# Moving the begin of 24 background weight-sum transfers out of the output projection

## The chip, the cores and the metric

The kernel runs on one core of a Trainium2 chip. The metric is the device time of one execution in microseconds. It is judged over several runs; one more execution was taken with the hardware profiler, and all rows below come from that one.

## The reference

One layer of a streaming encoder on x (1024 rows, 1024 columns, float32). Every product is done in float32 accuracy.

```python
h = rms_norm(x, ln1_g)
z = h @ w_in                         # columns for three mixers
y = concat(short_conv(...),          # gated 3-tap convolution, 256 columns
           diff_attention(...),      # 4 heads, block-causal, 512 columns
           gla(...))                 # gated linear attention, 4 heads, 256 columns
x = x + y @ w_out                    # output projection, 1024 x 1024
h2 = rms_norm(x, ln2_g)
x = x + square(relu(h2 @ w_mlp1)) @ w_mlp2    # 1024 -> 4096 -> 1024
```

## The kernel before

A float32 product is done as three fp32r products: `split` (L135) casts a tile to its high part on ScalarE (L136) and subtracts it from the original on VectorE for the low part (L137); `mm3` (L155) multiplies low by high, high by high, high by low. The two MLP products are done by a seven-product scheme on 2 x 2 blocks, in which the weight operand of a product is a block of w_mlp1 or w_mlp2 or a sum of such blocks. The sums don't depend on x. They are made by DMA alone, from DRAM to DRAM: one transfer copies 1 MB of a block, a later one adds 1 MB of another block onto it with `accum_op` (L116 and L119).

`BlockSums.steps()` (L111) is a generator over these transfers. For each of the two weights it gives 32 steps: 4 copies for sum 5, 4 copies for sum 2, 4 and 4 accumulations onto these, 4 copies and 4 accumulations for sum 4 (from sum 5), 4 copies and 4 accumulations for sum 1 (from sum 4). The copies for 5 and 2 read the weight, those for 4 and 1 read another sum. `sum_steps` (L125) chains the 32 of w_mlp1 and the 32 of w_mlp2, and the order is fixed. A step of w_mlp1 has rows of 8 KB, one of w_mlp2 rows of 2 KB.

`next_sum(when)` (L128) begins the next step: GpSimd copies one element of `when` into `paced`, which makes it wait until that element is written, and then issues the transfer from GpSimd's own queue (queue 0 in the profile). All other transfers are issued by SyncE, in order, on queue 1.

The stages, in order, and the steps that begin in each:

- The gate projection and the decay factors of the gated linear attention; the loop over 8 row tiles that makes `gv` (L354); its keys, states and queries. No steps.
- The gated linear loop, 16 iterations of `gla_scores` and `gla_out` (L497 to L501), with the projections of q, k and v for the first two attention heads interleaved (`steps01`). `gla_out` calls `next_sum` in each odd iteration: 8 steps.
- Four attention heads. Each calls `next_sum` after each of 8 query tiles (L609): 32 steps. Between the heads lie the projections that the next ones need.
- The convolution's projections, and the loads of y from DRAM (L671).
- The output projection (L724): four blocks of 256 columns of w_out, 8 row tiles each. A row tile is one `gemm_b` of 24 matmuls into a `ps_mm` bank (three of them), an addition to x1 on VectorE (L729) and a square with row sum on ScalarE (L730). In the first three blocks each row tile calls `next_sum` (L732): 24 steps. In the last block, each row tile is followed by `h2_tile` of that tile (norm, transposes, splits), and then come `h2_sums`.
- The first MLP product ("MLP 1", L831): 8 iterations of q, each with seven products of 24 matmuls each, their weight operands loaded by `w1_operand` (L757), two tiles of hidden units per iteration. No steps.
- The second MLP product (L928): seven terms in the order 5, 3, 7, 6, 4, 1, 2.

Weights are loaded by `load_w` (L139): two halves of 512 KB, each into a staging tile "st" (two of them, shared with `lp`, `g2` and the y loads), then split into tiles "hi" and "lo" (four each). `g2` (L698) is allocated in an "st" slot ahead of the output projection and read until the last `h2_tile`. A load waits for a free staging tile, a cast for a free hi tile. Tile's scheduler sets the order of each engine's instructions from a priority and its own model of times; dependencies become semaphore waits. `tc.issue_after` puts instructions of the same engine behind a given one.

Of the kernel before, what the change touches and what calls it, by code (L numbers as in the profile page):

```python
# [36 lines left out]
def hybrid_block(ctx, tc, x, ln1_g, w_in, conv_w, q_norm_g, k_norm_g, diff_lambda, diff_subln_g,  # L37
# [24 lines left out]
    def ps_tr():  # L62
        return psum.tile([P, 512], F32, name="ps_tr", tag="tr", bufs=2)
# [4 lines left out]
    def stage():  # L68
        return wpool.tile([P, 1024], F32, name="wst", tag="st", bufs=2)
# [58 lines left out]
    def next_sum(when):  # L128

        g = nc.gpsimd.tensor_copy(paced, when)  # L130
        with tc.issue_after(g.ins):
            next(sum_steps)


    def split(hi, lo, src):  # L135
        nc.scalar.copy(hi, src)  # L136
        return nc.vector.tensor_tensor(lo, src, hi.bitcast(F32), op=ALU.subtract)  # L137

    def load_w(w, c0, ncol):  # L139
        wb = []  # L140
        for kh in range(2):
            st = stage().rearrange("p (c n) -> p c n", c=4)
            wk = w[kh * 512:(kh + 1) * 512, :].rearrange("(c p) n -> p c n", p=P)
            nc.sync.dma_start(st, wk[:, :, c0:c0 + 256])
            hi = wpool.tile([P, 4, 272], F32R, name="whi", tag="hi", bufs=4)
            lo = wpool.tile([P, 4, 272], F32R, name="wlo", tag="lo", bufs=4)
            split(hi[:, :, 0:256], lo[:, :, 0:256], st)
            if ncol > 256:
                sx = c1.tile([P, 4, ncol - 256], F32, name="sx", tag="sx", bufs=2)
                nc.sync.dma_start(sx, wk[:, :, c0 + 256:c0 + ncol])  # L150
                split(hi[:, :, 256:ncol], lo[:, :, 256:ncol], sx)
            wb.append((hi, lo))
        return wb
# [19 lines left out]
    def gemm_b(wb, act, tt, ncol=256, ks=tuple(range(KC))):  # L173
        ps = ps_mm()
        th, o = tt // 4, (tt % 4) * P
        for kc in ks:
            hi, lo = wb[kc // 4]
            ah, al = act[th][kc // 4]
            mm3(ps[:, 0:ncol], ah[:, kc % 4, o:o + P], al[:, kc % 4, o:o + P],
                hi[:, kc % 4, 0:ncol], lo[:, kc % 4, 0:ncol], kc == ks[0], kc == ks[-1])  # L180
        return ps
# [29 lines left out]
    def g4(nm):  # L211
        return gp.tile([P, 1024], F32, name=nm, tag="g4", bufs=8)
# [110 lines left out]
    for j in range(4):  # L323
        ps = ps_s()
        for i in range(2):
            tt = 2 * j + i
# [13 lines left out]
    for pr in range(2):  # L340
        for th in range(2):
            ps = ps_s()
            for i in range(4):
                tt = th * 4 + i
# [8 lines left out]
    gv = r1.tile([P, NT, 256], F32, name="gv", tag="v")  # L353
    for tt in range(NT):  # L354
        ps = gemm_b(wb, hT, tt)
        nc.scalar.copy(gv[:, tt, :], ps[:, 0:256])
    wb = load_w(w_in, C_GK, 256)
    kE = [g4("kE") for _ in range(2)]
    for pr in range(2):
# [14 lines left out]
    for pr in range(2):  # L374
        nc.gpsimd.memset(S[pr][:, 0:64], 0.0)
        kv = [ps_s(), ps_s()]
        for c in range(15):
            tt, po = c // 2, (c % 2) * 64
# [82 lines left out]
    ssg = c1.tile([P, 32], F32, name="ssg")  # L461
# [12 lines left out]
    def gla_out(g):  # L474
        tt, hh = g // 2, g % 2
        po, att = hh * 64, attb[g % 4]
        ov = og[tt // 4][:, (tt % 4) * 256:(tt % 4) * 256 + 256].rearrange("p (r h e) -> p r h e", r=2, h=2)
        po_ = ps_tr()
        for pr in range(2):
            os_ = slice(pr * 64, (pr + 1) * 64)  # L480
            h0 = pr * P + hh * 64
            nc.tensor.matmul(po_[:, os_], att[:, pr, :], gv[:, tt, h0:h0 + 64], start=True, stop=False)
            for i in range(2):
                c = tt * 2 + i
                nc.tensor.matmul(po_[i * 64:(i + 1) * 64, os_],
                                 eb[pr][po:po + 64, c * 64:(c + 1) * 64],
                                 S[pr][po:po + 64, c * 64:(c + 1) * 64], start=False, stop=True)
        sq = gp.tile([P, P], F32, name="sqg", tag="sqg", bufs=2)
        nc.scalar.copy(ov[:, :, hh, :], po_[:, 0:P].rearrange("p (r e) -> p r e", r=2))
        nc.scalar.activation(sq, po_[:, 0:P], AF.Square)  # L490
        nc.vector.tensor_reduce(ssg[:, tt * 4:tt * 4 + 4].rearrange("p (r h) -> p r h", r=2)[:, :, hh],
                                sq.rearrange("p (r e) -> p r e", r=2), axis=AX.X, op=ALU.add)
        if g % 2 == 1:
            next_sum(ssg[0:1, tt * 4 + hh:tt * 4 + hh + 1])

    gla_scores(0)
    for g in range(2 * NT):  # L497
# [204 lines left out]
    ss2 = xp.tile([P, NT, 4], F32, name="ss2")  # L702

    def h2_tile(tt):
        r = norm_stats(ss2[:, tt, :], 4, xp)
        th, o = tt // 4, (tt % 4) * P
        osl = slice(o, o + P)
        for kh in range(2):
            ksl = slice(kh * 512, kh * 512 + 512)
            xn = xp.tile([P, 512], F32, name="xn", tag="xn", bufs=2)  # L710
            nc.vector.scalar_tensor_tensor(xn, x1[tt][:, ksl], r, g2[:, ksl], op0=ALU.mult, op1=ALU.mult)
            tp = ps_tr()
            for j in range(4):
                t_ = nc.tensor.transpose(tp[:, j * P:(j + 1) * P], xn[:, j * P:(j + 1) * P], ident)
            nc.scalar.copy(hb[th][kh][:, :, osl], tp.rearrange("p (c n) -> p c n", c=4))
        nc.sync.dma_start(x1d[tt], x1[tt])
        if th == 0:
            d6 = xp.tile([P, 4, P], F32, name="d6", tag="xn", bufs=2)
            nc.vector.tensor_tensor(d6, b11[:, :, osl], b21[:, :, osl], op=ALU.subtract)
            split(*[v[:, :, osl] for v in H[6]], d6)  # L720
            split(*[v[:, :, osl] for v in H[5]], b21[:, :, osl])
        return t_.ins

    for nb in range(4):  # L724
        wb = wo0 if nb == 0 else load_w(w_out, nb * 256, 256)
        for tt in range(NT):
            ps = gemm_b(wb, yT, tt, 256, (6, 7, 2, 3, 4, 5, 0, 1))
            xv = x1[tt][:, nb * 256:(nb + 1) * 256]
            nc.vector.tensor_tensor(xv, xv, ps[:, 0:256], op=ALU.add)  # L729
            nc.scalar.activation(ps[:, 0:256], xv, AF.Square, accum_out=ss2[:, tt, nb:nb + 1])  # L730
            if nb < 3:
                next_sum(ss2[0:1, tt, nb:nb + 1])  # L732
            if nb == 3 and tt < NT - 1:
                h2_tile(tt)

# [41 lines left out]
    def prods(q, i):  # L777
        w = w1_operand(q, i)
        return [prod(w, e, i, *BANKS[i]) for e in range(2)]
# [16 lines left out]
    def ftile(nm):  # L796
        return fp.tile([P, 512], F32, name=nm, tag=nm)
# [13 lines left out]
    def f_store(i, mp, r):  # L811
        nc.sync.dma_start(fdram[i][mp], r)
# [4 lines left out]
    def out65(mp, ps6, ps5):  # L817
        s6, s5, r5 = ftile("s6"), ftile("s5"), ftile("r5")
        nc.scalar.copy(s6, ps6)
        tadd(r5, ps5, s6)  # L820
        nc.scalar.copy(s5, ps5)
        relu2_v(r5)
        f_store(5, mp, r5)
        return s6, s5, r5
# [6 lines left out]
    for q in range(NQ):  # L831
        if q not in first:
            p6, p5 = prods(q, 6), prods(q, 5)
            first[q] = [out65(2 * q + e, p6[e], p5[e]) for e in range(2)]
        f = first.pop(q)
        p3 = prods(q, 3)
        s3s = []
        for e in range(2):
            s6, s5, r5 = f[e]
            s3 = ftile("s3")  # L840
            s3s.append(s3)
            nc.scalar.copy(s3, p3[e])
            tadd(s5, p3[e], s5, ALU.subtract)
        p7 = prods(q, 7)
        for e in range(2):
            s6, s5, r5 = f[e]
            tadd(s3s[e], p7[e], s3s[e])
            tadd(s6, s6, p7[e], ALU.subtract)
            relu2_s(s3s[e])
            f_store(3, 2 * q + e, s3s[e])  # L850
        p2 = prods(q, 2)
        for e in range(2):
            tadd(f[e][0], p2[e], f[e][0])
        p4 = prods(q, 4)
        for e in range(2):
            s6, s5, r5 = f[e]
            tadd(s6, p4[e], s6)
            tadd(s5, p4[e], s5)
            relu2_s(s6)
            f_store(7, 2 * q + e, s6)  # L860
        p1 = prods(q, 1)
        for e in range(2):
            s6, s5, r5 = f[e]
            s3, mp = s3s[e], 2 * q + e
            tadd(s5, p1[e], s5)
            relu2_v(s5)
            d6, d4, d2 = gtile(), gtile(), gtile()
            tadd(d6, s5, r5, ALU.subtract)
            f_store(6, mp, d6)
            tadd(s5, s5, s3, ALU.subtract)  # L870
            f_store(1, mp, s5)
            tadd(d4, r5, s5, ALU.subtract)
            f_store(4, mp, d4)
            tadd(d2, s6, d4, ALU.subtract)
            f_store(2, mp, d2)


    fp_cm.__exit__(None, None, None)
# [49 lines left out]
    for ip, (op, dests, done) in enumerate(plan):  # L928
        banks = [psum.tile([P, 512], F32, name="pso", tag=t, bufs=n) for t, n in sets[ip % 2]]
        for c in range(NC2):  # L930
            w, f = load2(op, c)
# [48 lines left out]
```

## Time and profile before

| | us |
|---|---|
| median of 3 runs | 1267.23 |
| lowest and highest of the runs | 1264.94, 1267.30 |
| the profiled execution, device time | 1265.83 |
| the profiled execution, span of its instructions | 1264.1 |

The span is what the rows below divide; all times of instructions count from its start. In a timeline row the first number is the start and the second the duration; in brackets stand the idle time of the engine before the instruction and what ended it. PE is TensorE's matmuls, PEld its weight loads, DVE VectorE, ACT ScalarE, POOL GpSimd, SP SyncE. A DMA issue takes part of a microsecond on the issuing engine; the transfer lands later.

### The profile page before, as it was taken

How to read it: one execution, taken by the hardware profiler on the slowest of the kernel's cores; microseconds unless marked ns; L12 is line 12 of the kernel's file. 1: busy time of each engine (PE TensorE's matmuls, PEld its weight loads, DVE VectorE, ACT ScalarE, POOL GpSimd, SP SyncE). 2: the span in 40 equal slices, each digit the busy share in tenths (PEclk: the TensorE clock that was granted, in tenths of full speed). 3: DMA queues.
4: the chain of work that ended last, by engine and by line, in shares of the span. 5: the costliest groups of instructions: out<-in, count | busy, mean ns of one | idle time of the engine just before them, and what ended most of it. 6: DMA issues, size and time to landing. Idle time of an engine off the chain costs nothing.

```text
span 1264.1 us, 17602 instructions
## 1 busy us (share of the span) xinstructions
PE 1197.6 (95%) x6803; PEld 1029.7 (81%) x6803; DVE 743.8 (59%) x1366; ACT 522.8 (41%) x1019; POOL 65.7 (5%) x147
## 2 busy tenths in 40 slices
PE   6999999999999999676689999999999999999998
PEld 6897899998988788576668888888888888888887
DVE  6616654568677873111597866776666555554553
ACT  6621233557566642111475343344433333333332
POOL 1000000020102112122000000000000000000000
PEclk8999999999999999778789999999999999999999
DMA  6211244197819778999734656565599995655000
GB/s 203 84 34 34 68 163 163 46 211 237 184 50 220 211 227 262 217 267 266 194 125 162 220 184 203 192 204 173 180 315 353 387 363 200 228 210 197 32 34 33
DMA packets 118961, 231.92 MB, mean 183 GB/s; under 512 B 7357, under 2 KB 53470, under 8 KB 115550
## 3 DMA queue, kind: packets, MB, share of 16 engines
q1 hardware_dynamic: 104286, 163.69, 38.1%
q0 software_dynamic: 14592, 67.11, 22.0%
q8 instruction: 53, 0.87, 0.3%
q14 instruction: 30, 0.25, 0.1%
HBM read 189.89 MB, written 108.00 MB: 236 GB/s over the span
## 4 chain that ended last, share of the span: by engine, by line
PE 78%; DMA 10%; DVE 6%; ACT 4%; issue 1%; SPq 1%; ACTq 0%; DVEq 0%
PE pso L158 8%; PE pso L156 8%; PE pso L157 8%; PE psp L156 8%; PE psp L157 8%; PE psp L158 8%; DMA wst<-in_w_out_dram 6%; PE ps_mm L156 6%; PE ps_mm L158 6%; PE ps_mm L157 6%; PE ps_av L605 3%; DMA wst<-in_w_mlp_dram 2%; PE ps_tr L597 1%; PE ps_s L575 1%; DMA wst<-ydram 1%; PE ps_s L576 1%
## 5 line engine op out<-in xcount | busy, mean ns | idle before, releaser
L157 PE MATMUL pso<-o2h 128*128 128x512 f32 x448 | 174.3, 389 | 0.0
L156 PE MATMUL pso<-o2l,o2h 128*128 128x512 f32 x448 | 174.3, 389 | 0.0
L158 PE MATMUL pso<-o2h,o2l 128*128 128x512 f32 x448 | 174.3, 389 | 0.0
L156 PE MATMUL ps_mm<-wlo,hTh 128*128 128x256 f32 (+1 forms) x512 | 147.8, 289 | 3.8 <-ACT hTh L201 3.8
L137 DVE TENSOR_TENSOR o2l<-f,o2h 128x1024 fp32r<-128x1024 f32 x56 | 68.6, 1225 | 139.4 <-ACT o2h L136 139.4
L157 PE MATMUL ps_mm<-whi,hTh 128*128 128x256 f32 (+1 forms) x512 | 147.1, 287 | 0.0
L158 PE MATMUL ps_mm<-whi,hTl 128*128 128x256 f32 (+1 forms) x512 | 146.2, 286 | 0.0
L136 ACT CAST o2h<-f 128x1024 fp32r<-128x1024 f32 x56 | 58.8, 1051 | 190.5 <-PE pso L157 186.6
L156 PE MATMUL ps_mm<-wlo,yTh 128*128 128x256 f32 x256 | 80.2, 313 | 32.5 <-ACT ps_mm L730 26.8
L137 DVE TENSOR_TENSOR wlo<-wst,whi 128x1024 fp32r<-128x1024 f32 x34 | 41.6, 1224 | 114.5 <-ACT whi L136 112.0
L136 ACT CAST w1h<-wst 128x1024 fp32r<-128x1024 f32 x56 | 58.9, 1053 | 106.8 <-PE psp L157 86.9
L156 PEld LDWEIGHTS ps_mm<-wlo,hTh 128*128 128x128 f32 x512 | 97.0, 190 | 7.0 <-ACT hTh L201 4.7
L157 PEld LDWEIGHTS pso<-o2h 128*128 128x128 f32 x448 | 84.1, 188 | 17.6
L158 PEld LDWEIGHTS pso<-o2h,o2l 128*128 128x128 f32 x448 | 84.1, 188 | 17.5
L156 PEld LDWEIGHTS pso<-o2l,o2h 128*128 128x128 f32 x448 | 84.1, 188 | 17.3
L158 PEld LDWEIGHTS ps_mm<-whi,hTl 128*128 128x128 f32 x512 | 97.4, 190 | 0.7 <-DVE hTl L202 0.2
L157 PEld LDWEIGHTS ps_mm<-whi,hTh 128*128 128x128 f32 x512 | 97.1, 190 | 0.9 <-issue 0.3
L815 DVE TENSOR_TENSOR s<-psp,s 128x512 f32<-128x512 f32 x96 | 64.7, 689 | 51.0 <-PE psp L158 46.0
L137 DVE TENSOR_TENSOR w1l<-wst,w1h 128x1024 fp32r<-128x1024 f32 x56 | 68.4, 1221 | 35.1 <-ACT w1h L136 35.1
L156 PEld LDWEIGHTS ps_mm<-wlo,yTh 128*128 128x128 f32 x256 | 55.5, 217 | 33.8 <-ACT ps_mm L730 27.9
L158 PE MATMUL ps_mm<-whi,yTl 128*128 128x256 f32 x256 | 78.3, 306 | 0.0
L157 PE MATMUL ps_mm<-whi,yTh 128*128 128x256 f32 x256 | 78.3, 306 | 0.0
(284 smaller groups left out, 2631.5 us busy)
## 6 DMA issues: line engine op xcount, KB each, us to landing
f<-fdram SPq DMA_DIRECT2D x28, 1024.0 KB
w1s<-in_w_mlp_dram POOLq DMA_DIRECT2D x24, 1024.0 KB, 9.8
w2s<-in_w_mlp_dram POOLq DMA_DIRECT2D x24, 1024.0 KB, 17.6
wst<-w1s SPq DMA_DIRECT2D x32, 512.0 KB
w<-w2s SPq DMA_DIRECT2D x16, 1024.0 KB
wst<-in_w_in_dram SPq DMA_DIRECT2D x26, 512.0 KB
wst<-in_w_mlp_dram SPq DMA_DIRECT2D x24, 512.0 KB
fdram<-s SPq DMA_DIRECT2D x48, 256.0 KB
```

The lines of the kernel that those rows point to most:

```text
L136: nc.scalar.copy(hi, src)
L137: return nc.vector.tensor_tensor(lo, src, hi.bitcast(F32), op=ALU.subtract)
L156: nc.tensor.matmul(ps, lh, rl, start=first, stop=False)
L157: nc.tensor.matmul(ps, lh, rh, start=False, stop=False)
L158: return nc.tensor.matmul(ps, ll, rh, start=False, stop=last)
L575: nc.tensor.matmul(ps[:, 0:w], qi, kll[c][:, j * 512:j * 512 + w], start=True, stop=False)
L576: nc.tensor.matmul(ps[:, 0:w], qi, khh[c][:, j * 512:j * 512 + w], start=False, stop=True)
L597: nc.tensor.transpose(tp[:, b * P:(b + 1) * P], pc[0][:, (b0 + b) * P:(b0 + b + 1) * P], ident)
L605: nc.tensor.matmul(av[:, 0:P], aT[:, b * P:(b + 1) * P], v[:, kb, hh * P:hh * P + P], start=(kb == 0), stop=(kb == i))
L815: nc.vector.tensor_tensor(dst, a_, b_, op=op)
```

## The change

The 24 calls of `next_sum` in the output projection are removed. 24 others are added: 8 in the loop that makes `gv`, one after each row tile's copy; 8 in the even iterations of the gated linear loop, which had them in the odd ones alone; and 8 in MLP 1, one at the end of each iteration of q. The element that paces a step of MLP 1 is one of r5 of the same iteration's first tile, which `out65` writes early in the iteration (for q of 0 and 1 ahead of the loop).

```diff
     for tt in range(NT):
         ps = gemm_b(wb, hT, tt)
         nc.scalar.copy(gv[:, tt, :], ps[:, 0:256])
+        next_sum(gv[0:1, tt, 0:1])
...
-        if g % 2 == 1:
-            next_sum(ssg[0:1, tt * 4 + hh:tt * 4 + hh + 1])
+        next_sum(ssg[0:1, tt * 4 + hh:tt * 4 + hh + 1])
...
             nc.scalar.activation(ps[:, 0:256], xv, AF.Square, accum_out=ss2[:, tt, nb:nb + 1])
-            if nb < 3:
-                next_sum(ss2[0:1, tt, nb:nb + 1])
             if nb == 3 and tt < NT - 1:
                 h2_tile(tt)
...
             tadd(d2, s6, d4, ALU.subtract)
             f_store(2, mp, d2)
+        next_sum(f[0][2][0:1, 0:1])
```

Since the order of the 64 steps is fixed, each stage gets other steps than before:

| stage | before | after |
|---|---|---|
| `gv` loop | none | 8 copies of w_mlp1 |
| gated linear loop | 8 copies of w_mlp1 | 8 accumulations, 4 copies from a sum, 4 accumulations of w_mlp1 |
| head 0 | 8 accumulations of w_mlp1 | 4 copies from a sum, 4 accumulations of w_mlp1 |
| head 1 | 4 copies from a sum, 4 accumulations of w_mlp1 | 8 copies of w_mlp2 |
| head 2 | 4 copies from a sum, 4 accumulations of w_mlp1 | 8 accumulations of w_mlp2 |
| head 3 | 8 copies of w_mlp2 | 4 copies from a sum, 4 accumulations of w_mlp2 |
| output projection | 16 accumulations, 8 copies from a sum of w_mlp2 | none |
| MLP 1 | none | 4 copies from a sum, 4 accumulations of w_mlp2 |

## Rows read from the trace of the kernel before

**Rows 1.** The page, its first line.

```profile
span 1264.1 us, 17602 instructions
```

**Rows 2.** The page, shares of the span in the chain that ended last.

```profile
PE 78%; DMA 10%; DVE 6%; ACT 4%; issue 1%; SPq 1%; ACTq 0%; DVEq 0%
```

**Rows 3.** That chain in order of time, 455 to 665 us: start, duration, what.

```profile
459.95 7.29 DMA wst<-ydram
...
481.68 3.75 DMA wst<-in_w_out_dram
...
487.85 18.66 DMA wst<-in_w_out_dram
...
508.91 11.98 DMA wst<-in_w_out_dram
...
611.86 1.05 ACT w1h L136
```

**Rows 4.** Waits, ScalarE 485 to 660, TensorE 485 to 615 us: total, times, longest.

```profile
ACT whi L136 <- DMA wst<-in_w_out_dram: 54.7, 6, 12.4
...
ACT w1h L136 <- DMA wst<-w1s: 9.9, 1, 9.9
...
PE ps_mm L156 <- ACT ps_mm L730: 26.8, 5, 7.0
```

**Rows 5.** Timelines of TensorE and ScalarE: projection's first matmul, 25th square.

```profile
480.21 0.27 PE L156 MATMUL ps_mm<-wlo,yTh 128*128 128x256 f32 x1
...
600.59 0.39 ACT L730 ACTIVATE ps_mm<-x 128x256 f32<-128x256 f32 x1 [1.27 <-DVE x L729]
```

**Rows 6.** Windows: length, PE, PEld, DVE, ACT, POOL busy (instructions), PEclk, DMA share, GB/s.

```profile
160.00:208.00 48.00, 48.00 (x407) 43.96 (x408) 24.25 (x62) 15.53 (x50) 4.48 (x11) 1.00 0.41 140
...
480.00:503.00 23.00, 23.00 (x194) 22.92 (x192) 6.43 (x12) 5.58 (x16) 6.95 (x12) 1.00 0.95 293
503.00:600.00 97.00, 64.47 (x438) 63.24 (x436) 13.78 (x24) 14.59 (x42) 17.15 (x35) 0.80 1.09 250
...
638.00:654.00 16.00, 10.47 (x54) 8.36 (x52) 16.00 (x38) 10.15 (x20) 0.00 (x0) 0.87 0.24 78
...
660.00:790.00 130.00, 130.00 (x569) 106.46 (x568) 93.73 (x126) 56.86 (x79) 0.00 (x0) 1.00 0.57 189
```

**Rows 7.** Timeline of GpSimd: first and last paced copy of eight, an accumulating step.

```profile
147.31 0.18 POOL L130 COPY paced<-ssg 1x1 f32<-1x1 f32 x1 [13.79 <-DVE ssg L491]
...
213.16 0.17 POOL L130 COPY paced<-ssg 1x1 f32<-1x1 f32 x1 [8.03 <-DVE ssg L491]
...
251.00 0.86 POOL L119 DMA_DIRECT2D w1s<-in_w_mlp_dram  x1 [0.27 <-issue]
```

**Rows 8.** DMA queues in 288:290, 292:294, 502:504 us: packets, MB, share of 16 engines.

```profile
q0 software_dynamic: 52, 0.39, 92.4%
q1 hardware_dynamic: 50, 0.10, 15.1%
...
q0 software_dynamic: 38, 0.20, 47.8%
...
q0 software_dynamic: 151, 0.30, 80.4%
q1 hardware_dynamic: 155, 0.16, 28.8%
```

**Rows 9.** Timeline of SyncE's queue: the issues of two v weights (two halves each).

```profile
169.99 3.19 SPq L144 DMA_DIRECT2D wst<-in_w_in_dram  x2
...
207.85 3.19 SPq L144 DMA_DIRECT2D wst<-in_w_in_dram  x2
```

**Rows 10.** Timeline of ScalarE: the first cast of each of these two weights.

```profile
205.52 1.05 ACT L136 CAST whi<-wst 128x1024 fp32r<-128x1024 f32 x1 [1.80 <-PE ps_mm L158]
...
233.07 1.05 ACT L136 CAST whi<-wst 128x1024 fp32r<-128x1024 f32 x1 [1.05 <-PE ps_mm L158]
```

**Rows 11.** Waits of ScalarE in MLP 1, 660 to 926 us.

```profile
ACT w1h L136 <- PE psp L157: 83.7, 47, 3.3
```

## The prediction

> **What bounds the kernel now.** I began with the page. The span is 1264.1 us [rows 1], and the chain that ended last is 78% TensorE and 10% DMA [rows 2]. A tenth of the span that waits for transfers in a kernel of matrix products is the thing to place, so I read the chain in order of time [rows 3]. Before 460 us it is TensorE, VectorE and ScalarE in turn. From 460 to 612 us it is almost nothing but loads: 7.29 us for a 512 KB piece of y, 3.75 us for the first w_out half that is loaded inside the stage, then 18.66, 11.98 and so on for halves of the same 512 KB. The reader is to see that one and the same kind of load takes 3.75 us once and 12 to 19 us afterwards.
>
> The waits say how this reaches TensorE [rows 4]. ScalarE stands before a cast of w_out for 54.7 us in six times, all on DMA, and 9.9 us once on an MLP operand. ScalarE works in order, so the squares of L730 stand behind such a cast; a square holds a PSUM bank of ps_mm, of which there are three; TensorE then waits for L730, 26.8 us in five times. The windows give the size [rows 6]: from 480 to 503 us TensorE is full (23.00 of 23 us, clock 1.00, 194 matmuls, so 0.1186 us each), from 503 to 600 us it has 64.47 of 97 us at a granted clock of 0.80. In that stretch DMA is at 1.09 and VectorE and ScalarE are below 15 us of 97. The projection is bound by its loads, and the loads by what shares the DMA engines: the 24 block sum steps that L732 issues.
>
> **What is removed.** The projection begins at 480.21 us [rows 5]. Were TensorE never short of weights, a row tile of one 256-column block is 24 matmuls of 0.1186 us, 2.85 us [rows 6]. ScalarE's cast at 611.86 us is the last that waits on a load [rows 3]; it is the second MLP operand's, and in ScalarE's order it stands behind the 25th square, which ran at 600.59 us [rows 5]. So I compare the time of that cast. Without competing transfers: 25 x 2.85 = 71.3 us brings the 25th tile to 551.5 us. The operand's own load can't begin earlier than the staging slot allows, and there is only one: g2 (L698) holds the other "st" slot through the whole stage. The first MLP operand is cast when the third block has freed its hi buffer, at 480.2 + 24 x 2.85 = 548.6 us; from there to the next issue it takes 2.4 us for cast and subtraction (the load issued at 487.85 us landed 18.66 us later, at 506.51, and the next was issued at 508.91 [rows 3]); then comes a load. For the load I take the 3.75 us of 481.68 us, which is the nearest uncrowded one of this very kind; the bound above is the 11.98 us of a crowded one. That gives 548.6 + 2.4 + 3.75 = 554.8 us, so 57.1 us are removed; 48.9 us with the bound above, and 60 us if the operand is there when the 25th tile is done.
>
> Do the other loads keep up, by the same price? A half costs 3.75 + 2.4 = 6.2 us, two halves 12.3 us, against 8 x 2.85 = 22.8 us of matmuls in a block. Yes, with 10 us over. The second half of block 1 is issued at 487.85 us behind eight x tiles, 4 MB on the same queue; it has until 503 us.
>
> From 612 us on the stage is the norm and the h2 sums. From 638 to 654 us VectorE is busy 16.00 of 16 us [rows 6], so this part doesn't shrink with faster loads. TensorE's clock there is 0.87, and full speed may give some 4 us in the 26 us ahead of it, an estimate from that clock; I take none.
>
> **What is added, stage by stage.** The order of the 64 steps is fixed, so 16 early begins shift everything behind them: the gv loop gets the 8 copies of w1's first two sums, the gated linear loop 8 accumulations, 4 copies and 4 accumulations of w1 where it had 8 copies, the attentions lighter and heavier mixes, MLP 1 the last 8 steps of w2.
>
> *Issue cost.* A step is a copy of one element and a DMA issue, under 1.4 us of GpSimd together, as the rows with POOL show [rows 7]. GpSimd has nothing else there that is waited for, so I put it at nothing; without that cover, 24 x 1.4 us = 34 us could be late, but only for other steps.
>
> *The gated linear loop.* In [rows 7] eight paced copies stand 9.4 us apart (147.31 to 213.16 us), so with twice as many a step will come every 4.7 us. An accumulation of w1 takes about 5.2 us of all DMA engines: the eight of head 0 were issued from 251.00 us and their queue runs empty in the window of 292 to 294 us [rows 7, 8]. The first eight therefore last from some 144 to 186 us; the next four from 199 to about 220 us. What suffers are the weight loads beside them. How much, a two-microsecond window shows: beside w1 accumulations queue 0 moved 52 packets and queue 1 moved 50, although those of queue 0 are 7.5 KB; beside w2 accumulations the counts are 151 and 155 [rows 8]. The two queues take turns by packet, whatever the size, so 1 KB packets of a load run at 25 per us beside w1 and 77 per us beside w2. The Trainium skill has this as a rule: in "DMA: Bandwidth & Descriptors", section "Queues, rings and completion order", each engine goes round its queue rows packet by packet. By that rule the trace agrees, and it speaks against this stage, since w1's packets are the largest that a load can meet.
>
> Worked out: the v load of pair 0 (two halves, 1024 packets) is issued from 169.99 us [rows 9]. Until 186 us it moves some 360 packets; the rest falls between copies and is through by about 190 us. Its cast comes at 205.52 us [rows 10]: 15 us to spare. The next pair's load, issued from 207.85 us [rows 9], moves 260 packets until 220 us and is through near 223 us; the cast is at 233.07 us [rows 10]: 10 us to spare. The four y stores of the loop queue behind it, and ScalarE may stand some 5 us before the third yt. Three ps_mm banks are 8.5 us of matmuls. So between nothing and 3 us; I take 1. TensorE is busy 48.00 of 48 us there now [rows 6], so any stall would be seen.
>
> *The attentions.* Head 0 and 1 get less accumulation than now. Head 3 now gets four accumulations as its last steps, where plain copies stood. They end later, and the y loads stand beside them: the 7.29 us load of 459.95 us [rows 3] already was beside copies. The last piece of y is needed almost when it arrives, so a delay goes to TensorE in full. Below: nothing, for the turns by packet cost 4 KB loads little. Above: two accumulations more to get past, 2 x 5.2 - 4 = 6 us. I take 1, nearer to nothing since the queues share.
>
> *MLP 1.* 569 matmuls in 130 us [rows 6] are 0.228 us each, so 5.5 us for an operand of 24. Eight steps are spread over some 270 us where DMA is at 0.57. The casts there wait for TensorE, not for loads: 83.7 us in 47 times [rows 11], so loads lie in their slots before a buffer is free, and four hi buffers are three operands, 16 us, ahead. A load beside a w2 accumulation takes 512/77 = 6.6 us plus its latency, about 8.7 us; that fits. Bounds 0 and 5 us; I take 0. The last sum is needed only by the sixth of the second product's seven terms.
>
> **Sum.** 57.1 - 1 - 1 = 55.1 us less. The profiled execution took 1265.83 us, so 1210.7; it lies between the lowest (1264.94) and the median (1267.23) of the runs. I say 1211 us.
>
> **Rivals.**
> *The receiving stages give back a part.* If accumulations ran without a gap, the two v loads would need 1024/25 = 41 us each: 3 us past the cast of the first pair and 16 us past the second's. With 6 us before the projection that is 25 us in place of the 2 I took, 1234 us. For it: the spare of 10 to 15 us rests on 5.2 us for an accumulation, against 4.7 us between steps. Against it: the loop's eight plus four accumulations end.
>
> *It doesn't do what it says.* One staging slot makes the loads a chain even alone. This decides once a half takes more than 22.8/2 - 2.4 = 9 us; at 11.98 us a block would take 28.8 us, and with halves as long as the 18.66 us behind x tiles 42.1 us. Three blocks of 42.1 us in place of 22.8 are 57.9 us, so the gain is gone and the time stays near 1266 us, within 0.2%; the x tiles and x1d stores would have to hold the loads there. Against it is the 3.75 us load. The Trainium skill's section "Issuing engines are not separate DMA queues" (same page) says that all such transfers share 16 engines, so the bytes are paid for somewhere; the windows show where there is room, 0.41 and 0.57 of DMA [rows 6].
>
> *Slower: MLP 1 stops on its casts.* There each operand's load is in ScalarE's order, as in the projection. If every one of the eight steps delayed one load from 3.75 to 11.98 us with no buffer between, 8 x 8.2 = 66 us would be lost, more than the 55 gained: 1277 us. It decides when the load's lateness exceeds the 16 us of operands ahead, or when ScalarE, held at a cast, keeps PSUM banks for over one product of 5.5 us. The 47 casts that wait for TensorE alone [rows 11] speak against it.
>
> **Chances.** The forecast 0.76, by itself 1204 to 1219 us; part given back 0.17; no gain 0.03; slower 0.04. A measurement of this kernel tells about 0.2% from no change: faster 0.93, same 0.03, slower 0.04. The ends: 60 us removed and nothing given back is 1206 us, 2 more from the clock 1204; 48.9 us removed and 9 given back (3 and 6; MLP 1 nothing) is 1226 us. I take 1204 to 1226 us, which leaves out the worse half of the second case and the last two.
>
> **What would show it.** Right: no wait of ScalarE on w_out over 4 us, squares 2.85 us apart through three blocks, granted clock near 1.00 from 480 to 550 us, second MLP operand cast near 555 us, MLP 1 steady some 55 us earlier. Gated linear loop: load casts still waiting for TensorE, with DMA near full to 186 us. Wrong: casts there or in MLP 1 that wait for DMA, TensorE idle before the projection, or loads of w_out still at 9 us or more.

## The result, and the profile after

The changed kernel takes 1223.72 us, the median of 4 runs (1220.67 to 1226.46), beside 1267.26 us for the kernel before beside it: a ratio of 0.966 with a 95% interval of 0.9634 to 0.9685. It is faster, by 43.5 us. The forecast was 1211 us with a range of 1204 to 1226 us, so the time lies inside the range and 12.7 us above the forecast. The profiled execution of the changed kernel took 1223.45 us.

The page of the kernel after, its first line and the shares of its chain, answers to [rows 1, 2]: transfers were 10% of the chain and are 3%.

```profile
span 1221.8 us, 17609 instructions
...
PE 85%; DVE 7%; ACT 3%; DMA 3%; issue 1%; SPq 1%; ACTq 0%
```

To see in which stage the time went I took landmarks that both kernels have. In the kernel after, these are the first and last starts of four groups of matmuls (duration minimum, median and maximum in ns; then first and last start in us):

```profile
L471 PE MATMUL ps_s<-eb,enb x64: 272/272/374, 141.8 to 206.9; 64*128 64x128 f32 x64
...
L575 PE MATMUL ps_s<-kll,qs x96: 221/397/500, 249.6 to 455.8; 128*128 128x512 f32 x48, 128*128 128x128 f32 x16, 128*128 128x256 f32 x16, 128*128 128x384 f32 x16
...
L156 PE MATMUL ps_mm<-wlo,yTh x256: 276/282/384, 490.0 to 587.5; 128*128 128x256 f32 x128
...
L156 PE MATMUL pso<-o2l,o2h x448: 388/389/628, 908.2 to 1217.1; 128*128 128x512 f32 x150
```

The first row's first start is where the gated linear loop begins, the second's where head 0 begins, the third's where the output projection begins, the fourth's first and last where the second MLP product begins and nearly ends. Their differences cut the span into five stretches. The same landmarks of every kernel of this study (us; the first column is the median device time, the others come from the one profiled execution):

| kernel | median | to the gated loop | gated loop | heads and y loads | projection and MLP 1 | second product |
|---|---|---|---|---|---|---|
| before | 1267.26 | 140.0 | 100.0 | 240.2 | 475.2 | 304.0 |
| after | 1223.72 | 141.8 | 107.8 | 240.4 | 418.2 | 308.9 |
| after, again | 1223.55 | 141.9 | 107.6 | 240.4 | 416.8 | 310.3 |
| y tile in og | 1215.71 | 141.1 | 100.1 | 240.3 | 417.6 | 309.6 |
| last step early | 1216.39 | 142.0 | 105.9 | 240.6 | 417.7 | 303.9 |
| both | 1211.69 | 143.0 | 100.0 | 240.5 | 417.8 | 304.0 |
| without the last 8 | 1216.49 | 142.1 | 106.1 | 240.4 | 417.5 | 304.0 |
| before without its 24 | 1210.29 | 142.2 | 100.1 | 240.1 | 417.0 | 304.0 |
| 8 in the first block | 1243.22 | 141.9 | 108.0 | 240.3 | 443.0 | 304.0 |
| w1 in 2 KB rows | 1224.03 | 142.2 | 109.0 | 240.5 | 417.6 | 308.7 |

The first two lines hold the whole result: 1.8 us more ahead of the gated loop, 7.8 us more in it, 0.2 us in the heads, 57.0 us less in the projection and MLP 1, and 4.9 us more in the second product. The sum is -42.3 us; the two profiled executions differ by 1265.83 - 1223.45 = 42.4 us.

**The projection.** The waits of the kernel after, ScalarE 485 to 660 us and TensorE in the same stretch (total, times, longest), answer to [rows 4]; the 54.7 us before casts of w_out are 7.6 us, and TensorE's 26.8 us are 0.5 us.

```profile
ACT whi L136 <- DMA wst<-in_w_out_dram: 7.6, 5, 2.7
...
PE ps_mm L156 <- ACT ps_mm L730: 0.5, 1, 0.5
```

ScalarE's timeline after, around the 25th square and the second MLP operand's cast, answers to [rows 3, 5]. The two squares are 2.85 us apart, as are all on the mean from 502.94 to 562.74 us (21 steps); where a cast stands between two of them it is up to 4.7 us (520.03 and 524.69 us). The cast comes 564.52 - 490.0 = 74.5 us after the projection's first matmul; before it was 611.86 - 480.21 = 131.65 us.

```profile
559.89 0.39 ACT L730 ACTIVATE ps_mm<-x 128x256 f32<-128x256 f32 x1 [0.20 <-DVE x L729]
...
562.74 0.39 ACT L730 ACTIVATE ps_mm<-x 128x256 f32<-128x256 f32 x1 [2.34 <-DVE x L729]
...
564.52 1.05 ACT L136 CAST w1h<-wst 128x1024 fp32r<-128x1024 f32 x1 [0.43 <-DMA wst<-w1s]
```

Windows of the kernel after (columns as in [rows 6], which they answer). From 513 to 559 us, TensorE is full at the full clock with DMA at 0.19. In MLP 1 it is busy 240.00 of 240 us. Two windows are not full: 228 to 234 us, and the one from 900 us on.

```profile
160.00:208.00 48.00, 48.00 (x407) 44.10 (x407) 23.45 (x62) 14.21 (x48) 9.88 (x22) 1.00 0.98 248
...
228.00:234.00 6.00, 2.11 (x15) 1.91 (x14) 0.00 (x0) 2.11 (x5) 0.00 (x0) 0.76 0.59 209
...
513.00:559.00 46.00, 46.00 (x390) 46.00 (x389) 11.40 (x20) 13.10 (x39) 0.00 (x0) 1.00 0.19 58
...
660.00:900.00 240.00, 240.00 (x1047) 196.39 (x1046) 161.51 (x213) 94.42 (x129) 6.14 (x12) 1.00 0.74 226
900.00:1000.00 100.00, 97.06 (x421) 79.76 (x420) 57.19 (x62) 36.33 (x38) 0.00 (x0) 0.98 0.99 366
```

**The gated loop's end.** The chain of the kernel after, in order of time, from 216 to 234 us (start, duration, what): TensorE is no longer on it, but a store of y for 14.71 us.

```profile
216.01 0.70 ACT yt L514
216.72 14.71 DMA ydram<-yt
231.51 0.57 ACT yt L514
...
232.81 0.27 ACT dv L437
233.13 0.58 PE ps_mm L156
```

Read backwards: a matmul waits for a PSUM bank that ScalarE frees (dv, L437); ScalarE is late because it stood at the third y tile (L514), of which there are two; the tile comes free when its store has ended. The waits of ScalarE and TensorE from 200 to 250 us, after, give the sizes:

```profile
ACT yt L514 <- DMA ydram<-yt: 11.8, 1, 11.8
...
PE ps_mm L156 <- ACT dv L437: 3.9, 1, 3.9
```

Why a 256 KB store lasts 14.7 us is read from two engines' issues and the queues. SyncE issued a v load at 211.19 us, and the store behind it on the same queue. GpSimd issued the first of four w1 accumulations at 203.27 us and the last at 216.97 us (timelines of SyncE and GpSimd, after):

```profile
203.27 0.84 POOL L119 DMA_DIRECT2D w1s<-in_w_mlp_dram  x1 [0.33 <-issue]
...
216.97 0.82 POOL L119 DMA_DIRECT2D w1s<-in_w_mlp_dram  x1 [0.32 <-issue]
...
211.19 3.18 SPq L144 DMA_DIRECT2D wst<-in_w_in_dram  x2
216.72 16.44 SPq L215 DMA_DIRECT2D ydram<-yt  x4
```

The queues of the kernel after from 218 to 220 us and from 228 to 230 us (packets, MB, share of 16 engines). While the accumulations run, queue 1 moves 48 packets in 2 us, beside 48 of queue 0; when they have ended, 509.

```profile
q0 software_dynamic: 48, 0.39, 94.2%
q1 hardware_dynamic: 48, 0.05, 9.0%
...
q1 hardware_dynamic: 509, 0.64, 94.5%
```

The Trainium skill, "DMA: Bandwidth & Descriptors", section "Queues, rings and completion order", has the turn by packet that this shows; the trace agrees, 48 to 48.

The 3.9 us are not all. In two later windows of the kernel after, TensorE is full at half the clock, 1.2 GHz, though it had full speed before it stood still:

```profile
235.00:237.00 2.00, 2.00 (x11) 2.00 (x11) 0.00 (x0) 0.00 (x0) 0.00 (x0) 0.50 0.00 0
237.00:239.00 2.00, 2.00 (x15) 2.00 (x15) 0.00 (x0) 0.37 (x1) 0.00 (x0) 0.75 0.00 0
```

The matmuls there start 0.21 us apart instead of 0.12, up to some 238 us: 22 matmuls take 4.9 us where 22 x 0.12 = 2.6 us would do, so about 2.3 us go to the clock. Of the 7.8 us, that leaves 1.6 us: from 140 to 150 us the granted clock of this execution is 0.83 with TensorE busy throughout, and (1 - 0.83) x 10 = 1.7 us. The second execution of the same kernel has 1.00 there, and a longer wait at the loop's end: ScalarE 12.5 us, TensorE 4.7 us.

**The second product's start.** Waits of ScalarE and TensorE in the kernel after, 880 to 930 us, and GpSimd's last step:

```profile
ACT o2h L136 <- DMA f<-fdram: 7.7, 1, 7.7
...
PE pso L156 <- DVE o2l L137: 2.9, 1, 2.9
...
881.02 1.02 POOL L119 DMA_DIRECT2D w2s<-in_w_mlp_dram  x1 [0.96 <-issue]
```

The eighth step of MLP 1 is an accumulation that begins at 881 us, early in the last iteration of q, beside the first loads of w2 and f for the next product, which SyncE issues at 880.20 and 882.93 us. The first cast of f then waits 7.7 us for its load; before it was 3.9 us, which TensorE did not notice. Of the 4.9 us TensorE stands 2.9 us, up to 916.81 us, and loses the rest behind that, at a granted clock of 0.50 from 918 to 920 us.

### The profile page after: what moved, and what is told of

It is laid out like the page before. It is cut to its first block, busy times and chain, and to the rows that moved or that the text cites. A ratio compares the mean times of both kernels' runs of the same rounds, so it can differ in the third digit from the quotient of the medians.

```text
span 1221.8 us, 17609 instructions
## 1 busy us (share of the span) xinstructions
PE 1189.3 (97%) x6803; PEld 1021.1 (84%) x6803; DVE 744.6 (61%) x1366; ACT 523.2 (43%) x1019; POOL 66.0 (5%) x147
## 4 chain that ended last, share of the span: by engine, by line
PE 85%; DVE 7%; ACT 3%; DMA 3%; issue 1%; SPq 1%; ACTq 0%
PE pso L158 8%; PE ps_mm L156 8%; PE pso L156 8%; PE pso L157 8%; PE psp L156 8%; PE psp L157 8%; PE psp L158 8%; PE ps_mm L158 8%; PE ps_mm L157 8%; PE ps_av L605 3%; PE ps_tr L597 1%; PE ps_s L575 1%; PE ps_s L576 1%; DMA ydram<-yt 1%; PE ps_s L471 1%
## 5 line engine op out<-in xcount | busy, mean ns | idle before, releaser
L137 DVE TENSOR_TENSOR o2l<-f,o2h 128x1024 fp32r<-128x1024 f32 x56 | 68.6, 1225 | 144.2 <-ACT o2h L136 144.2
L137 DVE TENSOR_TENSOR w1l<-wst,w1h 128x1024 fp32r<-128x1024 f32 x56 | 68.4, 1222 | 21.9 <-ACT w1h L136 21.8
L156 PE MATMUL ps_mm<-wlo,yTh 128*128 128x256 f32 x256 | 72.6, 284 | 0.5 <-ACT ps_mm L730 0.5
L158 PE MATMUL ps_mm<-whi,yTl 128*128 128x256 f32 x256 | 72.2, 282 | 0.0
L157 PE MATMUL ps_mm<-whi,yTh 128*128 128x256 f32 x256 | 72.2, 282 | 0.0
L137 DVE TENSOR_TENSOR o2l<-w,o2h 128x1024 fp32r<-128x1024 f32 x56 | 68.2, 1219 | 0.0
```

The lines of the kernel that those rows point to most:

```text
L156: nc.tensor.matmul(ps, lh, rl, start=first, stop=False)
L157: nc.tensor.matmul(ps, lh, rh, start=False, stop=False)
L158: return nc.tensor.matmul(ps, ll, rh, start=False, stop=last)
```

## The experiments

All are timed beside the kernel before on the same chip: the first four beside a median of 1265.35 us, the last four beside 1266.32 us.

**The y tile.** The loop's third and fourth y tiles are written into `og[0]`, which is no longer read by then, so that they need not wait for a store.

```diff
-            yt = y_tile()
+            yt = y_tile() if th == 0 else og[0][:, pr * 512:(pr + 1) * 512]
```

> The changed kernel, but the third and fourth y tile of the gated linear loop are written into og[0], which is free by then, so ScalarE no longer waits there for a y store to land. All 64 transfers begin where they did. Theory A: the 6 us lost at the end of this loop came from ScalarE standing 11.8 us at that one wait (3.9 us of TensorE and a lowered clock after it), so the time falls by 5 to 7 us from 1223.7, to about 1217.5, and no wait of ScalarE on a y store is left there. Theory B: TensorE lost the time to the crowded transfers themselves (weights late, or a clock that falls anyhow); then the wait only moves to the next cast and the time stays within 2 us of 1223.7.

Measured: 1215.71 us (1215.11 to 1217.04), ratio 0.9599 [0.9579, 0.9619]. That is 49.6 us less than the kernel before beside it, where the changed kernel has 43.5, so some 6 us are won, as theory A has it (5 to 7). The gated loop takes 100.1 us, as before the change (this execution also lacks the lower clock at 140 to 150 us), and its end is full at the full clock (window of this kernel, 228 to 234 us):

```profile
228.00:234.00 6.00, 6.00 (x53) 6.00 (x52) 0.00 (x0) 0.75 (x2) 0.00 (x0) 1.00 0.37 140
```

The accumulations, the v load and the store are still there, so it was the wait for the store at the y tile that cost TensorE the time at the loop's end, and not the crowded transfers themselves.

**The last step.** The eight steps of MLP 1 begin in the first seven iterations, two of them in the third.

```diff
-        next_sum(f[0][2][0:1, 0:1])
+        if q < NQ - 1:
+            next_sum(f[0][2][0:1, 0:1])
+        if q == 2:
+            next_sum(f[0][2][0:1, 0:1])
```

> The changed kernel, but the last of the eight steps in MLP 1 begins in the third iteration of q together with that one's own, and none in the last iteration. Theory A: the 4.8 us lost at the start of the second MLP product came from this one accumulation beside the first loads of f and of the weight sum, so the time falls by 3 to 5 us, to about 1219.5, and the first cast of f waits about 4 us instead of 7.7. Theory B: the loss there has another cause (the order of the stores and loads on the load queue), so the time stays within 2 us of 1223.7.

Measured: 1216.39 us (1216.2 to 1219.03), ratio 0.9608 [0.9587, 0.9628], 49.0 us less than the kernel before beside it, so some 5 us are won against the changed kernel, the upper end of theory A. The wait for f is 2.9 us and TensorE waits for nothing; the second product takes 303.9 us, as before. (The gated loop is 1.9 us shorter too, since this execution lacks the lower clock at 140 to 150 us.) Waits and a window of this kernel:

```profile
ACT o2h L136 <- DMA f<-fdram: 2.9, 1, 2.9
...
890.00:940.00 50.00, 50.00 (x222) 41.24 (x221) 29.26 (x35) 18.92 (x22) 0.00 (x0) 1.00 0.98 360
```

**Both edits together.**

> Both edits of the two runs above together. Theory A: the two losses are apart in time and add up, so about 11 us less, near 1213; this is the time that the changed kernel would have without the two waits. Theory B: at most the better of the two alone, not below 1218.

Measured: 1211.69 us (1211.59 to 1211.84), ratio 0.9566 [0.9547, 0.9585]. Both losses are gone at once: 53.7 us less than the kernel before beside it, 10 us more than the changed kernel wins, against the 11 us of theory A. It comes within 1 us of what was forecast for the changed kernel, with 3.0 us more ahead of the gated loop than the kernel before.

**Without the last eight.** The eight steps of MLP 1 are left out altogether, and the term that needs their sum reads another one, so this kernel doesn't compute the layer.

```diff
-        next_sum(f[0][2][0:1, 0:1])
...
-        nc.sync.dma_start(w, sums2.operand(i)[c * 512:(c + 1) * 512, :].rearrange("(j p) n -> p j n", p=P))
+        nc.sync.dma_start(w, sums2.operand(4 if i == 1 else i)[c * 512:(c + 1) * 512, :].rearrange("(j p) n -> p j n", p=P))
```

> The changed kernel without the eight transfers of MLP 1: they are left out, and the product that needs that sum reads the sum before it instead. Theory A: only the last of the eight costs anything, so the time is that of the run with the last step early, about 1219.5. Theory C: each of the eight costs TensorE something in MLP 1 through late operand loads; then the time falls by more than the last step's 5 us, below 1217.

Measured: 1216.49 us (1213.61 to 1219.32), ratio 0.9605 [0.958, 0.9629]. That is the time with the last step early, 1216.39 us. The other seven steps of MLP 1 cost nothing that is seen: 417.5 us for projection and MLP 1 against 417.7.

**The changed kernel once more**, as the yardstick for the kernels that run with it.

> The changed kernel itself, once more, so that the runs beside it have it on the same chip. Both theories: within 2 us of 1222 to 1224, with the same two waits (ScalarE on a y store for some 12 us, on f for some 8 us).

Measured: 1223.55 us (1220.76 to 1224.72), ratio 0.9655 [0.9635, 0.9676]. The two losses stand again: waits of 12.5 us at the y tile and 8.4 us at f.

**Before, without its 24.** From the kernel before, the 24 transfers of the projection are left out and put nowhere else. Of the sums of w_mlp2 only the first 8 copies are then made, and two terms read another sum, so this kernel doesn't compute the layer either.

```diff
-            if nb < 3:
-                next_sum(ss2[0:1, tt, nb:nb + 1])
...
-        nc.sync.dma_start(w, sums2.operand(i)[c * 512:(c + 1) * 512, :].rearrange("(j p) n -> p j n", p=P))
+        nc.sync.dma_start(w, sums2.operand(5 if i in (1, 4) else i)[c * 512:(c + 1) * 512, :].rearrange("(j p) n -> p j n", p=P))
```

> The kernel before without the 24 transfers of the output projection: they are left out, nothing is put elsewhere, and the products that need those two sums read another sum instead. Theory A (the projection was bound by loads that shared the DMA engines with these 24): 55 to 59 us less than the kernel before, about 1208, TensorE full through three blocks; so the change gives the whole of this and loses some 12 us in other stages. Theory D (one staging slot makes the loads a chain anyway): less than 40 us of gain.

Measured: 1210.29 us (1207.29 to 1211.29), ratio 0.955 [0.9529, 0.957], 56.0 us less than before. The removal by itself, with no other stage touched, is worth what the sum gave it; projection and MLP 1 take 58.2 us less. Windows of this kernel over the projection's first three blocks (columns as in [rows 6]):

```profile
480.00:503.00 23.00, 23.00 (x186) 22.52 (x185) 8.33 (x14) 7.24 (x18) 0.00 (x0) 1.00 0.67 253
503.00:549.00 46.00, 46.00 (x390) 46.00 (x389) 11.60 (x21) 12.76 (x38) 0.00 (x0) 1.00 0.19 58
```

The 97 us window of [rows 6], with its 64.47 us of matmuls at a clock of 0.80, is thus the transfers' doing, and the one staging slot that `g2` leaves is enough.

**Eight in the first block.** Is the projection's first block, which was full in [rows 6], room for the last eight steps? They are taken out of MLP 1 and put there.

```diff
             nc.scalar.activation(ps[:, 0:256], xv, AF.Square, accum_out=ss2[:, tt, nb:nb + 1])
+            if nb == 0:
+                next_sum(ss2[0:1, tt, nb:nb + 1])
...
-        next_sum(f[0][2][0:1, 0:1])
```

> The changed kernel, but the last eight steps begin in the first block of the output projection instead of MLP 1. Theory A: four copies and four accumulations are some 34 us of all DMA engines from 490 us on, so the loads of the second and third block come late there; this costs 8 to 14 us, and the 5 us at the start of the second MLP product are saved: 3 to 9 us slower than the changed kernel. Theory E (a few transfers fit into the slack of 10 us that each block has): not slower, some 5 us faster.

Measured: 1243.22 us (1242.44 to 1244.12), ratio 0.9814 [0.9795, 0.9833]: 19.7 us above the changed kernel, where 3 to 9 us were expected. Projection and MLP 1 lose 26.2 us (443.0 against 416.8), and the second product gets its 6.3 us back. The direction held; the size was far off. The chain of this kernel shows one load of 30.16 us, and TensorE waited for its split 17.2 us in one piece. In the changed kernel the same load, issued at 498.38 us behind the eight x tiles, was cast at 510.14 us, 11.8 us later.

```profile
498.52 30.16 DMA wst<-in_w_out_dram
...
PE ps_mm L156 <- DVE wlo L137: 17.2, 1, 17.2
...
508.00:531.00 23.00, 5.93 (x51) 5.73 (x49) 1.59 (x3) 1.55 (x3) 2.26 (x3) 0.72 0.96 238
```

The x tiles ahead of the load and the load itself meet first the four copies from sum to sum, issued from 499.93 to 504.15 us, and then two of the four accumulations (508.25 and 511.51 us); the other two are issued at 532.78 and 534.00 us, when the load has landed, and meet the next ones. The queues from 506 to 508 us:

```profile
q0 software_dynamic: 32, 1.05, 129.7%
q1 hardware_dynamic: 32, 0.12, 14.6%
```

Again turn by turn, 32 to 32, but a packet of queue 0 is 1.05 MB / 32 = 33 KB on the mean here, and queue 1 gets a tenth of the bytes. How much of the delay the copies cost and how much the accumulations, no run separates.

**w1 sums in 2 KB rows.** The sums of w_mlp1 are cut by columns, so that the rows of a step are as short as those of w_mlp2.

```diff
-            self.rows = [slice(i, i + step) for i in range(0, r, step)]
+            if c > 512:
+                self.rows = [(slice(0, r), slice(i, i + 512)) for i in range(0, c, 512)]
+            else:
+                self.rows = [(slice(i, i + step), slice(0, c)) for i in range(0, r, step)]
```

> The changed kernel with the sums of w_mlp1 cut by columns instead of rows: each step still moves 1 MB, in rows of 2 KB instead of 8 KB (and the copies from a sum no longer contiguous). Theory P (queues take turns by packet): at the end of the gated linear loop the load of the next v weight gets about 77 packets per us instead of 25, lands by about 226 us and the y store behind it soon after; ScalarE's wait for it falls from 12 to 4 to 8 us and the time by 3 to 5 us. Theory Q (only the bytes in flight count): the wait stays at 11 to 13 us and the time within 2 us of the changed kernel.

Measured: 1224.03 us (1222.39 to 1224.74), ratio 0.9657 [0.9638, 0.9676], the time of the changed kernel. So far theory Q is right. The packets did what was to be tested: queue 1 gets three times as many turns (queues of this kernel, 218 to 220 us), and yet the third y tile waits longer, 13.5 us, than under either theory:

```profile
q0 software_dynamic: 152, 0.30, 82.2%
q1 hardware_dynamic: 150, 0.15, 27.9%
...
ACT yt L517 <- DMA ydram<-yt: 15.3, 2, 13.5
```

Queue 0 moves 0.30 MB in these 2 us where it moved 0.39, and it still moves 0.25 MB from 234 to 236 us, where it had ended by 228 us. What the loads gain in turns, they lose in the time that they must share. The packet rate was the right rule for the rate and the wrong lever. The edit cuts the copies from a sum too; GpSimd waits 3.6 us for two of them ahead of the accumulations, and the first of these is issued at 204.23 us instead of 203.27.

## Why the prediction was right, and where its sum was off

| term of the sum | forecast, us | measured, us |
|---|---|---|
| projection (measured together with MLP 1) | -57.1 | -57.0 |
| gated linear loop | +1 | +7.8 (7.6 in the second execution) |
| attentions and y loads | +1 | +0.2 |
| MLP 1 (measured at the start of the second product) | 0 | +4.9 |
| ahead of the gated loop | none | +1.8 |
| sum | -55.1 | -42.3 |

**What is removed: right, and for the reason given.** "Right: no wait of ScalarE on w_out over 4 us, squares 2.85 us apart through three blocks, granted clock near 1.00 from 480 to 550 us" holds with 2.7 us, 2.85 us on the mean, and 1.00. The step by the second operand's cast held to a tenth, 74.5 us from the projection's start against 554.8 - 480.2 = 74.6, and not by errors that cancel: the first operand's cast is at 558.64 us, 68.6 us after the start (68.4 in the working), the next load is issued at 560.98 us, 2.3 us behind it (2.4), and its cast follows 3.5 us later (3.75). Taking the price of the uncrowded load rather than the bound of 11.98 us was right; the kernel before without its 24 transfers shows the gain alone. The one half behind the x tiles, which the working left without a price, was cast 11.8 us after its issue, just in time for the end of its block (490.0 + 22.8 = 512.8 us).

**"So between nothing and 3 us; I take 1": the mechanism right, the size wrong.** The prediction named the place, four y stores queued behind the second pair's v load and ScalarE standing before the third y tile, and the cover, three banks or 8.5 us. But "some 5 us" was 11.8 us, above the cover, and TensorE stood 3.9 us. Two numbers of the working were short. The four accumulations were to end at about 220 us, 12 us after the v load's issue at 207.85 us; they kept queue 0 to some 228 us, 17 us after its issue at 211.19 us, and only then went queue 1 from 48 packets in 2 us to 509. And the price of an idle TensorE was taken as its idle time: the clock fell to 1.2 GHz behind it, some 2.3 us more. The Trainium skill, "TensorE: Matmul & The Clock Gate", section "Part 1: The HAM clock gate (the "warmup" mystery)", says that the clock is lowered unless activity releases it; the 0.50 behind the idle stretch agrees, and the 0.50 from 146 to 148 us, with TensorE busy, is not explained by it. The load casts themselves, which the first rival put at stake, waited only for TensorE there, as predicted. So part of that rival came true by another way, the store, and not by the 25 us that it gave. (In its sum, 169.99 + 41 is 5 us past the first cast at 205.52 us, not 3.) And w1's packets are not "the largest that a load can meet": those of the copies from sum to sum are 33 KB on the mean against 8.

**"I take 0" for MLP 1: right for MLP 1, wrong at its edge.** TensorE is full there, 240.00 of 240 us, and casts wait for TensorE (70.1 us in 38 times from 660 to 930 us, answering to [rows 11]). The prediction's own sign of being wrong, casts in MLP 1 that wait for DMA, did show: three of them, 4.7 us together, where the kernel before had none from 660 to 926 us; TensorE did not stand for it. I spread eight steps "over some 270 us" and asked when their sum is needed, the sixth term of the second product. I did not ask where the last step falls: into the last iteration, at 881 us, on the loads of w2 and f with which the next product begins. That is 4.9 us, and the kernel with the last step early has none of it.

**"I take 1" for the y loads: smaller.** The heads and y loads together take 0.2 us more, and all of it lies behind the heads: from the last score matmul (L575) to the projection it is 490.0 - 455.8 = 34.2 us, and 34.0 us before. So the four accumulations at the end of head 3 cost almost nothing.

**What was in no term.** 1.8 us ahead of the gated loop and 1.7 us inside it are stretches of lower granted clock. The first stands at 50 to 60 us, ahead of the first moved transfer at 62.7 us, and the kernel before without its 24 transfers, which moves none, has 142.2 us to the gated loop. So it is not the change that brings the first; for the one at 140 to 150 us, which only two executions of the changed kernels have, the cause stays open.

**The time against the range.** The prediction gave 1204 to 1219 us to its forecast alone. 1223.7 us lies above that, and inside the whole range only because this took in ends at which something is given back. The sum is 12.8 us short: 6.8 us in the gated loop, 4.9 us at the last step and 1.8 us ahead of the loop, less 0.8 us at the y loads, with 0.1 us in the projection.

## What to carry to other kernels

A background transfer taken off a stage is worth what that stage's own chain says, and it is worked out well by following one late instruction (here a cast) with the durations of an uncrowded load. Where transfers are put, look at two places that a mean of DMA share hides: a store that queues behind a load on the same issuing queue and holds a small ring of tiles, and the last step of a stage, which meets the first loads for the next. Where TensorE's cover is nearly as long as the wait, price the crossing at idle time plus a stretch at half the clock, and prefer to remove the wait (a tile from a buffer that has gone dead) to tuning the transfers.

## What the runs showed of the hardware that was not expected

- A copy from one sum to another moves in far larger packets than one of a weight: 32 packets for 1.05 MB in 2 us, while queue 1 beside it gets 32 packets for 0.12 MB. A copy of a weight in 2 KB rows moved 153 packets for 0.60 MB (320 to 322 us of the changed kernel). A load that met four copies from sum to sum and two accumulations took 30.16 us; in the changed kernel, without them, it was cast 11.8 us after its issue.
- Beside an accumulation in 2 KB rows another queue gets 150 packets in 2 us, against 48 beside one in 8 KB rows, but the accumulation takes longer: its queue moved 0.30 MB in 2 us against 0.39 MB.
- After 3.9 us of idle time TensorE ran at 0.50 of its clock for nearly 5 us (233.13 to some 238 us) with its matmuls back to back, 0.21 us apart instead of 0.12.
- The granted clock fell to 0.50 for single windows of 2 us (146 to 148 us in the changed kernel) with TensorE busy 2.00 of 2 us, in one execution and not in the other of the same kernel (1.00 there).
